# The gated convolution of a decoder trunk: c and v gates with activations held and 512 features streamed, the product turned through DRAM, and the b gate moved behind them

## The chip, the cores and the metric

The kernel runs on one core of one Trainium2 chip. The metric is device time in microseconds (us) of one execution; the median of three runs of the kernel before is 950.28 us (950.25 to 950.47). Five engines work from in-order instruction queues and meet at semaphores: TensorE (PE in the profile, its weight loads PEld), VectorE (DVE), ScalarE (ACT), GpSimd (POOL) and SyncE (SP), which here issues nearly all transfers.

## The reference

One sequence of 256 tokens with 1024 features passes two layers. Each is a half-step SwiGLU FFN (2816 hidden), a mixer, and a second half-step FFN, each behind an RMS norm and added to the residual `h`. The mixer of the second layer is a sparse attention, which the change does not touch; that of the first is the short gated convolution:

```python
def short_conv_mixer(x, w_in, conv_w, w_out):
    b_gate, c_gate, v = jnp.split(x @ w_in, 3, axis=-1)
    u = c_gate * v
    y = lax.conv_general_dilated(u, conv_w[:, None, :], window_strides=(1,),
                                 padding=[(CONV_WIDTH - 1, 0)], ...
                                 feature_group_count=D_MODEL)
    return (b_gate * y) @ w_out
```

`x` is the RMS-normed `h`; `w_in` is 1024 x 3072, and the convolution has three taps per feature, which look back over 0, 1 and 2 tokens. Everything is float32.

## The kernel before, in words

**Products.** A float32 product is made of float32r parts: each operand is split into a rounded high half and the low rest, and hi·hi, lo·hi and hi·lo are summed in PSUM. Weights come from DRAM in chunks of 128x2048 floats (`ws`, three buffers), and each half of a chunk is one *unit* of 128x1024: ACT casts it to the high half `wh` (L166), DVE subtracts to the low half `wl` (L183). Six units of each can be ready ahead. `W.take()` hands out the next one, `W.done()` says that PE is through with one and lets the stream *pump* the next (a cast on ACT, a subtraction on DVE) at that point of both queues.

**Two forms of a product.** In the *token form* (`ffn_tokens`, L432 to L434) the activations are held in the array, 128 tokens at a time, and 512 features of the weights stream past; the result has tokens on partitions. In the *feature form* (`a_pass`, L351 and L356) 128x128 weights are held and both halves of the activations, 512 wide, stream past (L351), then the high half alone, 256 wide, past the low weights (L356); the result has features on partitions, 256 tokens on the free axis.

**The convolution.** The residual lies with features on partitions, so in the kernel before all three gates are made in the feature form, for 128 features `f` at a time: eight rounds, each of three PSUM banks (c, v and b), three units of weights and 24 + 24 matmuls. After each round `conv_evac` makes what the next product needs: ACT copies and DVE adds the two halves of c and v (L365, L366), POOL multiplies them and scales by the squared inverse RMS (L718, L719), ACT and DVE do the same for b (L721, L722), POOL scales it (L723), ACT and DVE apply the taps (L727 to L729), DVE multiplies by b (L731), and `split` (L359 on ACT, L360 on DVE) leaves the two halves `zs[f]`. Between these steps `weave` pumps weights, so their casts and subtractions stand among them in the queues.

**After it.** `out_proj(zs, 1.0, nm)` is a feature-form product with four PSUM banks at its head: on the first three columns `zs[0]` to `zs[6]` are used, on the fourth `zs[0]` and `zs[1]`, and only then `zs[7]` and the rest (`cut = (7, 7, 7, 2)`). So PE asks for `zs[6]` six matmuls after the head's start, and for `zs[7]` when all 23 + 23 matmuls of the head are done.

**What sets the order.** The order is written out by hand in Python: every engine takes its instructions in the order in which the program text issues them, and a stream pump stands exactly where `W.done`, `W.pump`, `W.high` or `W.low` is called. All transfers named here stand in SP's one queue.

## Time and profile before

| what | us |
|---|---|
| median of the runs | 950.28 |
| the profiled execution, its own time | 950.93 |
| its span, first to last instruction | 949.1 |
| PE busy in the span | 944.6 |
| DVE busy | 657.5 |
| ACT busy | 532.4 |
| POOL busy | 138.8 |
| convolution's three gates on PE | 186.33 to 253.30 |
| head of its output product on PE | 253.30 to 264.45 |

Busy times are unions, so overlapping instructions of an engine count once. The last two rows are from the chain of waits, whose pieces follow each other without overlap; a matmul's own duration in other views is longer than the step from one to the next, since matmuls are pipelined. Steps from start to start are read from the timeline. Positions in us count from the start of the span.

### The profile page before, as it was taken

The page shows a single profiled execution, that of the slowest core. Times are in us where ns is not written, and L with a number is a line of the kernel's source. Part 1 is how long each engine was busy: PE and PEld are TensorE (multiplying, and loading weights), DVE is VectorE, ACT ScalarE, POOL GpSimd, SP SyncE. Part 2 cuts the span into 40 slices and gives each one's busy share as a digit, 9 for nine tenths or more (in the row PEclk, how much of TensorE's full clock was granted, in tenths as well). Part 3 has the DMA queues.
Part 4 walks back from the last instruction along what each step waited for, and adds up shares of the span by engine and source line. Part 5 has one row for each costly group of instructions (what it writes and reads, how often), then busy time and mean ns, then how long its engine had stood idle before and what let it go on. Part 6 is the DMA issues. An engine that isn't in the chain of part 4 may idle for free.

```text
span 949.1 us, 12899 instructions
## 1 busy us (share of the span) xinstructions
PE 944.6 (100%) x4674; PEld 792.3 (83%) x4674; DVE 657.5 (69%) x1058; ACT 532.4 (56%) x895; POOL 138.8 (15%) x215
## 2 busy tenths in 40 slices
PE   9999999999999999999999999999999999999998
PEld 7888888888888888888888888888877888888887
DVE  7766665778896677647756676865679786776662
ACT  7554544555565455545647774644589764544450
POOL 2000000244520010001221022200238120000000
PEclk9999999999999999999999999999999999999999
DMA  7778876645546998777646977876511247998770
GB/s 312 237 228 279 253 258 219 228 171 200 181 165 233 267 292 253 225 269 222 222 159 207 276 229 248 271 251 191 212 50 32 103 177 233 275 284 260 232 268 23
DMA packets 154380, 206.35 MB, mean 217 GB/s; under 512 B 115740, under 2 KB 131228, under 8 KB 133837
## 3 DMA queue, kind: packets, MB, share of 16 engines
q1 hardware_dynamic: 154172, 205.27, 66.3%
q8 instruction: 37, 0.61, 0.2%
q10 hardware_dynamic: 144, 0.26, 0.1%
q14 instruction: 27, 0.21, 0.1%
HBM read 189.75 MB, written 15.24 MB: 216 GB/s over the span
## 4 chain that ended last, share of the span: by engine, by line
PE 99%; DMA 1%; ACT 0%; SPq 0%; issue 0%; DVE 0%
PE mm L432 16%; PE mm L434 16%; PE mm L433 16%; PE a L533 7%; PE mm L351 4%; PE a L351 4%; PE a L539 4%; PE mm L493 3%; PE mm L494 3%; PE mm L495 3%; PE a L592 2%; PE a L590 2%; PE a L591 2%; PE mm L656 2%; PE a L356 2%; PE mm L356 2%
## 5 line engine op out<-in xcount | busy, mean ns | idle before, releaser
L183 DVE TENSOR_TENSOR wl<-ws,wh 128x1024 fp32r<-128x1024 f32 x316 | 390.5, 1255 | 209.4 <-ACT wh L166 192.2
L166 ACT CAST wh<-ws 128x1024 fp32r<-128x1024 f32 x316 | 324.6, 1048 | 219.7 <-DMA ws<-in_ffn_w_in_dram 99.0
L432 PE MATMUL mm<-wh,xs 128*128 128x512 f32 x656 | 256.2, 391 | 0.0
L434 PE MATMUL mm<-wl,xs 128*128 128x512 f32 x656 | 255.7, 390 | 0.0
L433 PE MATMUL mm<-wh,xs 128*128 128x512 f32 x656 | 255.6, 390 | 0.0
L434 PEld LDWEIGHTS mm<-wl,xs 128*128 128x128 f32 x656 | 123.2, 188 | 26.2 <-DVE wl L183 0.4
L433 PEld LDWEIGHTS mm<-wh,xs 128*128 128x128 f32 x656 | 123.3, 188 | 25.2
L432 PEld LDWEIGHTS mm<-wh,xs 128*128 128x128 f32 x656 | 123.3, 188 | 25.1
L311 POOL TENSOR_TENSOR sq<-sq,t 128x256 f32<-128x256 f32 x42 | 34.8, 829 | 384.6 <-ACT t L309 383.9
L390 ACT ACTIVATE t<-mm,rc 128x256 f32<-128x256 f32 x86 | 40.6, 472 | 56.2 <-DVE t L391 47.6
L533 PE MATMUL a<-act,wh 128*128 128x512 f32 x296 | 69.5, 390 | 0.0
L533 PEld LDWEIGHTS a<-act,wh 128*128 128x128 f32 x296 | 55.0, 188 | 10.9
L391 DVE SCALAR_TENSOR_TENSOR t<-mm,rc,t 128x256 f32<-128x256 f32 x86 | 41.4, 482 | 15.5 <-ACT t L390 12.0
L493 PE MATMUL mm<-wh,act 128*128 128x512 f32 x132 | 51.4, 390 | 0.0
L494 PE MATMUL mm<-wh,act 128*128 128x512 f32 x132 | 51.4, 389 | 0.0
L495 PE MATMUL mm<-wl,act 128*128 128x512 f32 x132 | 51.4, 389 | 0.0
L359 ACT CAST act<-t 128x256 fp32r<-128x256 f32 x96 | 34.6, 405 | 26.3 <-DVE t L731 19.4
L294 ACT ACTIVATE xs<-base 128x256 fp32r<-128x256 f32 x48 | 24.1, 505 | 43.0 <-DVE base L455 27.3
L392 DVE STREAM_TRANSPOSE t<-t 128x256 f32<-128x256 f32 x88 | 39.2, 445 | 3.1
L360 DVE TENSOR_TENSOR act<-t,act 128x256 fp32r<-128x256 f32 x96 | 37.1, 424 | 4.4 <-ACT act L359 4.4
L539 PEld LDWEIGHTS a<-act,wl 128*128 128x128 f32 x296 | 37.2, 192 | 1.0
L539 PE MATMUL a<-act,wl 128*128 128x256 f32 x296 | 37.5, 283 | 0.0
(279 smaller groups left out, 1203.6 us busy)
## 6 DMA issues: line engine op xcount, KB each, us to landing
ws<-in_ffn_w_in_dram SPq DMA_DIRECT2D x84, 1024.0 KB, 5.7
ws<-in_ffn_w_out_dram SPq DMA_DIRECT2D x44, 1024.0 KB, 6.2
ws<-in_conv_w_in_dram SPq DMA_DIRECT2D x12, 1024.0 KB, 4.6
turn<-t SPq DMA_DIRECT2D x44, 256.0 KB, 2.2
t<-turn SPq DMA_DIRECT2D x44, 256.0 KB, 7.2
ws<-in_w_kv_dram SPq DMA_DIRECT2D x6, 1024.0 KB, 5.8
ws<-in_conv_w_out_dram SPq DMA_DIRECT2D x4, 1024.0 KB, 5.0
ws<-in_attn_w_q_dram SPq DMA_DIRECT2D x4, 1024.0 KB, 4.9
```

Source lines behind the costliest of these rows:

```text
L166: ac.copy(h, src)
L183: ve.tensor_tensor(out=l, in0=src, in1=h.bitcast(F32), op=ALU.subtract)
L351: pe.matmul(o, u[0][:, k * P:(k + 1) * P], xs[k], start=(k == 0), stop=False)
L391: ve.scalar_tensor_tensor(out=s, in0=o[tt][:, T:], scalar=rc[:, tt:tt + 1], in1=s, op0=ALU.mult, op1=ALU.mult)
L432: pe.matmul(o[tt], sh, wh, start=(k == 0), stop=False)
L433: pe.matmul(o[tt], sl, wh, start=False, stop=False)
L434: pe.matmul(o[tt], sh, wl, start=False, stop=(k == 7))
L493: pe.matmul(o[:, tt], sh, wh, start=(k == 0), stop=False)
L494: pe.matmul(o[:, tt], sl, wh, start=False, stop=False)
L495: pe.matmul(o[:, tt], sh, wl, start=False, stop=(k == NF - 1))
L533: pe.matmul(o, run[k][0], lhs[k], start=(k == 0), stop=(k == last))
L539: pe.matmul(o[:, :T], run[k][1], lhs[k][:, :T], start=False, stop=(k == last))
```

## The change

The c and v gates are now made in the token form, 512 features at a time, in four groups: c of features 0 to 511, v of the same, then c and v of features 512 to 1023. ACT copies the two banks of c out (L787). DVE multiplies v's banks by them and by the squared inverse RMS of each token (L735), turns 32x32 blocks (L737), and SP writes the result to DRAM and reads it back with features on partitions (L738, L745). The inverse RMS is still made as a row (L331); for the token scale its first row goes through DRAM into a column (L768, L769), and POOL squares that (L770). Taps (L756 on ACT, L758 twice on DVE) and the scaling by the inverse RMS (L760 on POOL) follow from the turned `u`: features 0 to 511 during the fourth group, the rest behind the matmuls of b's rounds 4 to 6. The b gate then runs in the feature form alone, eight rounds of one bank, one unit and 8 + 8 matmuls. The weights are packed to fit, and two of the attention's bias rows are loaded by one transfer in place of two.

```diff
-    def conv_evac(f, ocv, ob, R, R2, zs):
-        r = total(ocv, 2)
-        yield
-        u = mk([P, 768], "pr", 6)[:, :T + 2]
-        po.memset(u[:, :2], 0.0)
-        po.tensor_tensor(out=u[:, 2:], in0=r[:, 0], in1=r[:, 1], op=ALU.mult)
-        po.tensor_tensor(out=u[:, 2:], in0=u[:, 2:], in1=R2, op=ALU.mult)
...
+    def conv_tokens(o, step):
+        for k in range(8):
+            if k % 2 == 0:
+                u, = W.take()
+            wh, wl = [u[x][:, (k % 2) * 512:(k % 2 + 1) * 512] for x in range(2)]
+            for tt in range(2):
+                sh, sl = xs[k][:, tt * P:(tt + 1) * P], xs[k][:, T + tt * P:T + (tt + 1) * P]
+                pe.matmul(o[:, tt], sh, wh, start=(k == 0), stop=False)
+                pe.matmul(o[:, tt], sl, wh, start=False, stop=False)
+                pe.matmul(o[:, tt], sh, wl, start=False, stop=(k == 7))
+            if k % 2 == 1:
+                W.done()
+            step(k)
+    def conv_turned(gate, o):
+        d = mk([2, 2, P, T], "conv", 2, pool=dr)
+        for tt in range(2):
+            tb = t2()
+            ve.scalar_tensor_tensor(out=gate[tt], in0=o[:, tt], scalar=conv["r2"][:, tt:tt + 1], in1=gate[tt],
+                                    op0=ALU.mult, op1=ALU.mult)
+            ve.transpose(tb, gate[tt])
+            sy.dma_start(d[:, tt].rearrange("m p n -> p m n"), tb.rearrange("p (m n) -> p m n", m=2))
+        return d
+    def conv_placed(d):
+        r = []
+        for m in range(2):
+            r.append(t2([P, 2, T]))
+            sy.dma_start(r[m].rearrange("p c (b j) -> p c b j", j=32),
+                         d[m].rearrange("t (b i) (x c j) -> (i x) c (t b) j", i=32, c=2, j=32))
+        return r
+    def conv_taps(f):
+        m, c = divmod(f, 2)
+        if c == 0:
+            Y.append(act([P, 2, T], F32))
+        tap = [gt[:, G_CONV + 8 * a + f:G_CONV + 8 * a + f + 1] for a in range(3)]
+        u, y = conv["u", m // 2][m % 2][:, c], Y[m][:, c]
+        ac.activation(y, u, AF.Copy, scale=tap[2])
+        for a in range(2):
+            ve.scalar_tensor_tensor(out=y[:, 2 - a:], in0=u[:, :T - 2 + a], scalar=tap[a], in1=y[:, 2 - a:],
+                                    op0=ALU.mult, op1=ALU.add)
+        po.tensor_tensor(out=y, in0=y, in1=conv["R"], op=ALU.mult)
+        if f % 4 == 3:
+            del conv["u", m // 2]
+    def conv_step(n, k):
+        if n == 0 and k == 5:
+            conv["R"] = R = nm.rows()
+            rd, rc, conv["r2"] = mk([1, T], "rd", 1, pool=dr), mk([P, 2], "rc", 2, pool=tiny), sm([P, 2])
+            sy.dma_start(rd, R[:1])
+            sy.dma_start(rc, rd.rearrange("o (t p) -> (o p) t", t=2))
+            po.tensor_tensor(out=conv["r2"], in0=rc, in1=rc, op=ALU.mult)
+        if n == 1 and k == 1:
+            next(tab)
+        if n == 2 and k == 3:
+            conv["u", 0] = conv_placed(conv.pop(("d", 0)))
+        if n == 3:
+            if 3 <= k < 7:
+                conv_taps(k - 3)
+            elif k == 7:
+                next(tab)
+    for n in range(4):
+        o = bank2()
+        conv_tokens(o, lambda k: conv_step(n, k))
+        if n % 2 == 0:
+            gate = [t2() for _ in range(2)]
+            for tt in range(2):
+                ac.copy(gate[tt], o[:, tt])
+        else:
+            conv["d", n // 2] = conv_turned(gate, o)
+            del gate
+    for f in range(8):
+        o, (u,) = bank(), W.take()
+        a_pass([(o, u, xs, range(8))])
+        W.done(1, False)
+        if f == 1:
+            conv["u", 1] = conv_placed(conv.pop(("d", 1)))
+        for x in {4: (4, 5), 5: (6,), 6: (7,)}.get(f, ()):
+            conv_taps(x)
         b = t1()
-        ac.copy(b, ob[:, T:])
-        ve.tensor_tensor(out=b, in0=ob[:, :T], in1=b, op=ALU.add)
-        po.tensor_tensor(out=b, in0=b, in1=R, op=ALU.mult)
...
+        ac.copy(b, o[:, T:])
+        ve.tensor_tensor(out=b, in0=o[:, :T], in1=b, op=ALU.add)
+        W.pump(1)
+        ve.tensor_tensor(out=b, in0=b, in1=Y[f // 2][:, f % 2], op=ALU.mult)
+        zs.append(act())
+        split(b, zs[f])
+        W.pump()
...
-            if a == 0 or j < 6:
+            if a == 0 or j < 4:
```

What this does to the queues is seen at three places. The first is DVE's queue in a round of the b gate. Before, one round `f` of all three gates stood there so (`mm` holds c and v, `a` holds b, `pr` is u, `wl` a weight unit's low half, `act` the half of `zs` that DVE writes):

```order
L366 TENSOR_TENSOR t_342_1834<-mm_1785,t_342_1834 128x512
L183 TENSOR_TENSOR wl_1841<-ws_1677,wh_1837 128x1024
L722 TENSOR_TENSOR t_347_1847<-a_1784,t_347_1847 128x256
L183 TENSOR_TENSOR wl_1853<-ws_1760,wh_1851 128x1024
L728 SCALAR_TENSOR_TENSOR t_350_1855<-pr_1843,base,t_350_1855 128x256
L729 SCALAR_TENSOR_TENSOR t_350_1855<-pr_1843,base,t_350_1855 128x256
L183 TENSOR_TENSOR wl_1863<-ws_1760,wh_1859 128x1024
L731 TENSOR_TENSOR t_350_1855<-t_350_1855,t_347_1847 128x256
L360 TENSOR_TENSOR act_1866<-t_350_1855,act_1866 128x256
```

Now round 5 of the b gate stands so (`act_2208` and `act_2171` are tiles of `Y`, `t_395` is u as it came back):

```order
L758 SCALAR_TENSOR_TENSOR act_2208<-t_395_2081,base,act_2208 128x254
L758 SCALAR_TENSOR_TENSOR act_2208<-t_395_2081,base,act_2208 128x255
L801 TENSOR_TENSOR t_420_2213<-a_2191,t_420_2213 128x256
L183 TENSOR_TENSOR wl_2220<-ws_2088,wh_2216 128x1024
L803 TENSOR_TENSOR t_420_2213<-t_420_2213,act_2171 128x256
L360 TENSOR_TENSOR act_2223<-t_420_2213,act_2223 128x256
```

A round has one weight unit in place of three and a third of the matmuls; rounds 0 to 3 and 7 lack the two L758, round 4 has four of them.

The second place is DVE's queue where the v gate of the second half ends and the b gate begins. Ahead of these rows stand, for features 0 to 511, two groups of four L758 with a weight subtraction between them. Of the kernel before nothing answers to it; there the round shown first repeats.

```order
L183 TENSOR_TENSOR wl_2018<-ws_1925,wh_2014 128x1024
L272 TENSOR_TENSOR act_2021<-t_342_1788,act_2021 128x128
L735 SCALAR_TENSOR_TENSOR t_368_1929<-mm_1933,sm_1744,t_368_1929 128x512
L737 STREAM_TRANSPOSE t_386_2026<-t_368_1929 128x512
L735 SCALAR_TENSOR_TENSOR t_369_1930<-mm_1933,sm_1744,t_369_1930 128x512
L737 STREAM_TRANSPOSE t_387_2030<-t_369_1930 128x512
L801 TENSOR_TENSOR t_389_2051<-a_2034,t_389_2051 128x256
L183 TENSOR_TENSOR wl_2056<-ws_1964,wh_2054 128x1024
L803 TENSOR_TENSOR t_389_2051<-t_389_2051,act_1968 128x256
```

The evacuation of the fourth group (L735, L737) thus stands ahead of the first round of b, and the taps of the first half ahead of both.

The third place is SP's queue. Before, in this stretch it held the loads of the weights alone, one behind the other; now the second half of the turn stands among them:

```order
L139 DMA ws_2016<-in_conv_w_out_dram 128x2048
L738 DMA conv_2025<-t_386_2026 128x2x256
L738 DMA conv_2025<-t_387_2030 128x2x256
L745 DMA t_394_2079<-conv_2025 128x16x32
L745 DMA t_395_2081<-conv_2025 128x16x32
L139 DMA ws_2088<-in_conv_w_out_dram 128x2048
L139 DMA ws_2146<-in_conv_w_out_dram 128x2048
```

Three of the four chunks of the output product's weights are loaded behind the two writes and two reads.

## The prediction

> **What bounds the kernel now.** I read the page's busy shares and chain first, then the chain within the convolution, then the queues of DVE, ACT and POOL there.

> ```profile
> PE 944.6 (100%) x4674; PEld 792.3 (83%) x4674; DVE 657.5 (69%) x1058; ACT 532.4 (56%) x895; POOL 138.8 (15%) x215
> ...
> PE 99%; DMA 1%; ACT 0%; SPq 0%; issue 0%; DVE 0%
> ```

> PE is the chain nearly everywhere: what the change saves on PE is saved, and what makes PE wait is lost. The chain in the convolution, one whole round and then the head of the output product (start, us, what, count):

> ```profile
> 203.26 3.65 PE mm L351 x16
> 206.91 1.81 PE a L351 x8
> 208.72 1.91 PE mm L356 x16
> 210.64 0.96 PE a L356 x8
> ...
> 253.30 5.24 PE a L351 x23
> 258.54 2.75 PE a L356 x23
> 261.29 0.23 PE a L351
> ```

> The pieces abut: no wait. c and v cost 3.65 + 1.91 = 5.56 a round, b 1.81 + 0.96 = 2.77. A 512-wide step takes 5.24/23 = 0.228. The first matmul that needs `zs[7]` starts at 261.29. When is that half written?

> ```profile
> 260.52 0.43 DVE L360 TENSOR_TENSOR act<-t,act 128x256 fp32r<-128x256 f32 x1 [0.47 <-ACT act L359]
> ```

> At 260.95, 7.65 behind the last gate matmul's end at 253.30, and 0.34 ahead of its use. So the tail of this stage already has almost no slack: what counts is when the last `zs` are written.

> **What PE saves.** The token form stands in the next FFN; 29 steps lie between these two rows of the timeline:

> ```profile
> 278.21 0.39 PE L432 MATMUL mm<-wh,xs 128*128 128x512 f32 x1
> ...
> 284.78 0.39 PE L434 MATMUL mm<-wl,xs 128*128 128x512 f32 x1
> ```

> A step is 6.57/29 = 0.2266. c and v become 4 x 48 = 192 of them, 43.5; before they were 8 x 5.56 = 44.5. The saving is **1.0 us**: as many columns stream, in fewer matmuls. b keeps its 8 x 2.77 = 22.2, and the two row-sum matmuls stay. Call E the end of the fourth token group on PE; PE then ends b at E + 22.2 and wants `zs[6]` six steps into the head, at E + 22.2 + 1.37 = **E + 23.5**.

> **What the other engines must do by then.** The units of work, from the same stage, first DVE with POOL quiet on its scaling, then with POOL at work (start, us; starts give the steps):

> ```profile
> 200.71 0.49 DVE L728 SCALAR_TENSOR_TENSOR t<-pr,base,t 128x256 f32<-128x256 f32 x1 [1.08 <-ACT t L727]
> 201.24 0.48 DVE L729 SCALAR_TENSOR_TENSOR t<-pr,base,t 128x256 f32<-128x256 f32 x1
> 201.65 1.22 DVE L183 TENSOR_TENSOR wl<-ws,wh 128x1024 fp32r<-128x1024 f32 x1
> 202.79 0.42 DVE L731 TENSOR_TENSOR t<-t,t 128x256 f32<-128x256 f32 x1
> 203.68 0.43 DVE L360 TENSOR_TENSOR act<-t,act 128x256 fp32r<-128x256 f32 x1 [0.47 <-ACT act L359]
> ...
> 205.12 1.64 DVE L183 TENSOR_TENSOR wl<-ws,wh 128x1024 fp32r<-128x1024 f32 x1 [0.26 <-ACT wh L166]
> 206.68 0.41 DVE L722 TENSOR_TENSOR t<-a,t 128x256 f32<-128x256 f32 x1
> 207.01 1.33 DVE L183 TENSOR_TENSOR wl<-ws,wh 128x1024 fp32r<-128x1024 f32 x1
> 208.27 0.96 DVE L728 SCALAR_TENSOR_TENSOR t<-pr,base,t 128x256 f32<-128x256 f32 x1
> 209.26 0.48 DVE L729 SCALAR_TENSOR_TENSOR t<-pr,base,t 128x256 f32<-128x256 f32 x1
> ```

> ```profile
> 200.10 0.73 POOL L723 TENSOR_TENSOR t<-t,R 128x256 f32<-128x256 f32 x1
> ...
> 207.22 1.72 POOL L723 TENSOR_TENSOR t<-t,R 128x256 f32<-128x256 f32 x1
> ```

> The same tap takes 0.49 at 200.71, and 0.96 where POOL's scaling runs to 208.94; the weight subtraction 1.22 or 1.64. Each stretches POOL too, 0.73 to 1.72. Steps: two taps 201.65 - 200.71 = 0.94, or 1.39 beside POOL (0.99 + 0.40); a subtraction 1.14, or 1.56 beside POOL; the add from PSUM 0.33; the multiply 0.42 and 0.04 to ACT. The ACT side:

> ```profile
> 243.63 0.41 ACT L359 CAST act<-t 128x256 fp32r<-128x256 f32 x1 [2.74 <-DVE t L731]
> 243.94 0.29 ACT L271 CAST act<-t 128x128 fp32r<-128x128 f32 x1
> ...
> 245.58 0.37 ACT L721 COPY t<-a 128x256 f32<-128x256 f32 x1
> 245.84 1.06 ACT L166 CAST wh<-ws 128x1024 fp32r<-128x1024 f32 x1
> ```

> Split cast to the next 0.31, copy to the next 0.26, weight cast 1.05. Other pieces, from the groups of the stage (count, busy us, mean ns of one), and two transposes from the timeline:

> ```profile
> L183 DVE TENSOR_TENSOR wl<-ws,wh 128x1024 fp32r<-128x1024 f32 x23 | 31.8, 1381 | 2.3 <-ACT wh L166 2.3
> ...
> L366 DVE TENSOR_TENSOR t<-mm,t 128x512 f32<-128x512 f32 x8 | 5.5, 684 | 0.8 <-ACT t L365 0.5
> ...
> L331 DVE RECIPROCAL R<-t 128x256 f32<-128x256 f32 x1 | 1.8, 1753 | 3.1 <-ACT t L329 3.1
> ...
> L272 DVE TENSOR_TENSOR act<-t,act 128x128 fp32r<-128x128 f32 x1 | 0.3, 289 | 0.0
> ```

> ```profile
> L727 ACT ACTIVATE t<-pr,base 128x256 f32<-128x256 f32 x7 | 3.6, 510 | 8.5 <-POOL pr L719 8.5
> ```

> ```profile
> 157.83 1.31 DVE L501 STREAM_TRANSPOSE pr<-mm 128x512 f32<-128x512 f32 x2
> ```

> **DVE at E.** In the fourth token group a unit of weights is freed each 12 steps = 2.72, and its cast and subtraction stand behind that. The one freed at E - 5.44 is cast in 1.05 and subtracted in 1.22, so DVE gets to the taps at E - 3.2. From there its queue holds, with POOL scaling each finished feature (L760) beside the next instruction: taps 0.94 + 1.39, subtraction 1.56, taps 2.33, subtraction 1.56, the table's L272 0.25 (0.29, less the overlap of the next start). Sum 8.0: it is done at **E + 4.8**. Behind it stands the evacuation of the fourth group, which the trace lacks in this shape: a multiply of 128x512 from PSUM is nearest to L366, 0.72 with its step, and two transposes to L501's 1.31; 2 x 0.72 + 1.31 = 2.75. DVE comes to the first round of b at **E + 7.6**, 4.8 after PE ended that round.

> **The rounds of b.** The queues make a ring: ACT copies b (L800), casts a weight; DVE, which added the copy in the meantime, subtracts that weight, multiplies by Y (L803); ACT casts the split, and only then copies the next round, which stands behind it. One turn: 0.26 + 1.05 + 0.04 + 1.14 + 0.46 + 0.31 = **3.26**, where PE makes a round in 2.77. Before, the three weights per round ran in the shadow of 8.33 us of matmuls; now each `zs` waits for one. Rounds 5 and 6 carry one feature's taps, round 4 two: ACT's tap 0.55, taps 0.94, add 0.33, subtraction beside POOL 1.56, 0.46, 0.31 make 4.15; with a second pair at 1.39 it is 5.54.

> First split cast: E + 7.6 + 0.33 + 1.14 + 0.46 = E + 9.5. Rounds 1 to 3 add 9.8, round 4 5.5, rounds 5 and 6 8.3: E + 33.1, and 0.86 later (203.68 + 0.43 - 203.25, where ACT had begun) `zs[6]` is whole: **E + 34.0**. PE waits 34.0 - 23.5 = **10.5 us** in the head, in pieces, since `zs[4]` and `zs[5]` are late too. `zs[7]` comes one turn later, 3.3, behind 17 x 0.228 + 2.75 = 6.6 of matmuls: covered.

> **Costed at nothing.** The scale's column: it is asked for by DVE at the end of the second group, 21.8 after the start; R starts at 36 steps, 8.2, and has a square root, the reciprocal's 1.75 and two small transfers to pass. Transfers of the turn's shapes (KB, median us to landing):

> ```profile
> back<-pr SPq DMA_DIRECT2D x6, 256.0 KB, 2.2
> t<-back SPq DMA_DIRECT2D x6, 256.0 KB, 6.0
> ```

> At about 2.2 each that is near 8.2 + 3 + 4.4 = 16, so 6 us of cover; gone, DVE would stall. On SP two waits stand ahead of weight loads, but six ready units are 16 us of PE. The turn's transfers: `back` and its return are the same shapes; the second half is written at E + 7.6 + 2.2, back 6.0 later, by E + 16 or, with a second issue held up, E + 20; its taps start at E + 19.6. ACT's copies of c (L787) run behind a whole group. The bias edit moves one transfer that only POOL awaits.

> **Sum.** -1.0 + 10.5 = **+9.5**. The span goes from 949.1 to 958.6, that execution from its own 950.93 to 960.4; it lies 0.65 above the median shown, so the median goes from 950.28 to **959.8**.

> **Bounds.** Lower: POOL never in the way. Three tap pairs and five subtractions up to `zs[6]` lose 0.45 and 0.42 each, 3.45: a wait of 7.0, +6.0, 956.3. Upper: the second half of the turn comes late as well (below) and every plain subtraction takes the stage's mean of 1.38: 0.16 more in four rounds, 0.6, with the full lock's 2.4 (below) and the transfer's 1.6: +14.1, 964.4. I take the middle, since the contended rows are this stage's own.

> **Rivals.** *The wait is absorbed.* DVE's whole work in the convolution hardly changes, and PE has four banks for b: if what DVE owes at E were worked off earlier, PE would keep its pace and only the saving would show: 949.3, within 0.2% (1.9 us, about what a measurement of this kernel can tell from no change). Against it: the ring alone, with no debt and no taps, puts `zs[6]` at E + 2.8 + 1.9 + 6 x 3.26 + 0.86 = E + 25.1, a wait of 1.6 and +0.6. It decides only where the ring turns in under 3.0.

> *A full lock.* If DVE stood still for the whole of POOL's instruction, 0.73, and not the 0.45 that rows lose, eight collisions would add 8 x 0.3 = 2.4: +11.9, 962.2. For it: POOL's 1.72 contains a DVE instruction entire. Against: 0.96 - 0.49 = 0.47. [...]

> *The turn is late.* The reads are the longest issues on SP:

> ```profile
> L508 SPq DMA_DIRECT2D t<-back x6: 591/1834/4294, 161.8 to 653.0; - x6
> ...
> DMA to landing us min/median/max: 2.1/5.1/7.1
> ```

> If the second read of the second half is issued 4.3 late and lands after 7.1, it is there at E + 9.8 + 4.3 + 7.1 = E + 21.2, 1.6 behind the time when its taps could start: +11.1, 961.4. Against: only round 5's features lie in that tile.

> **Chances.** Forecast as summed, between the bounds: 0.72. Full lock 0.10, turn late 0.08, both on the slow side. Absorbed to within 0.2%: 0.05; faster, where PE's step in the token form fell further than the FFN's: 0.03; the ring alone, +0.6, is within the 0.05; 0.02 for a larger loss that I don't see. Slower 0.92, same 0.05, faster 0.03. Range 955.5 to 964.0.

> **What would show it.** Right: in the chain, PE waits in L351 of the head for `act` from DVE, some 10 us in three or four pieces; DVE first comes to L801 some 7 to 8 after the fourth group's end; L803 to L803 is 3.2 to 3.3 in rounds 1 to 3, 4 to 5.6 in rounds 4 to 6; the token groups take 10.9 each. Wrong: no such wait in the head, PE waiting in a token group for weights or a bank, or DVE waiting for a transfer in L756 or L758.

## The result: 12.3 us slower, where 9.5 were forecast

The changed kernel takes 962.65 us (median of four runs, 961.83 to 963.21), the kernel before 950.38 beside it: a ratio of 1.0128 (95% interval 1.0110 to 1.0146). The forecast was 959.8, in a range of 955.5 to 964.0. The profiled execution took 962.77 (its span is 961.0), 11.84 more than the execution profiled before (950.93). From here on the working goes by these two.

The page, its busy shares and its row of the granted clock:

```profile
PE 948.0 (99%) x4610; PEld 791.2 (82%) x4610; DVE 655.0 (68%) x1058; ACT 532.6 (55%) x891; POOL 111.1 (12%) x191
...
PEclk9999999999899999999999999999999999999999
```

PE's busy time went up, though it has 64 matmuls fewer (4674 before), and one slice of the clock's row is no longer a 9. First the stage's borders, from PE's timeline, where c's first token matmul, b's first matmul and the head stand:

```profile
186.15 0.40 PE L724 MATMUL mm<-wh,xs 128*128 128x512 f32 x1
...
229.96 1.98 PE L351 MATMUL a<-xs,wh 128*128 128x512 f32 x8
...
232.73 0.63 PE L351 MATMUL a<-xs,wh 128*128 128x512 f32 x2
...
251.33 1.11 PE L356 MATMUL a<-xs,wl 128*128 128x256 f32 x8
252.61 1.21 PE L351 MATMUL a<-act,wh 128*128 128x512 f32 x4 [0.17 <-DVE t L801]
255.46 0.79 PE L351 MATMUL a<-act,wh 128*128 128x512 f32 x1 [1.64 <-DVE act L360]
259.66 0.80 PE L351 MATMUL a<-act,wh 128*128 128x512 f32 x1 [3.40 <-DVE act L360]
263.83 6.53 PE L351 MATMUL a<-act,wh 128*128 128x512 f32 x17 [3.38 <-DVE act L360]
270.20 2.92 PE L356 MATMUL a<-act,wl 128*128 128x256 f32 x23
```

The same two borders in the kernel before:

```profile
186.17 0.63 PE L351 MATMUL mm<-xs,wh 128*128 128x512 f32 x2
...
252.18 1.12 PE L356 MATMUL a<-xs,wl 128*128 128x256 f32 x8
253.13 0.63 PE L351 MATMUL a<-act,wh 128*128 128x512 f32 x2
```

E is 229.96. The first round of b takes 232.73 - 229.96 = 2.77, the seven behind it 2.79 each: the last one's low products begin at 251.33 and need 0.95 (before, 252.18 to 253.13), so that without a wait the head would begin at 252.28. That is 66.13 behind the stage's start, where the kernel before needed 66.96: a saving of 0.83. PE wants `zs[6]` 1.37 later, at 253.65, and goes on at 263.83: it lost 10.18. And then something that no step of the forecast holds: the 17 matmuls behind the last wait take 270.20 - 263.83 = 6.37, 0.375 a step in place of 0.228, which is 2.49 more than 3.88. The sum: -0.83 + 10.18 + 2.49 = **11.84**, the whole difference. From 270.20 on the steps are those of before.

DVE's queue from the fourth group on, from its timeline:

```profile
226.77 2.27 DVE L758 SCALAR_TENSOR_TENSOR act<-t,base,act 128x254 f32<-128x254 f32 x4
228.97 1.21 DVE L183 TENSOR_TENSOR wl<-ws,wh 128x1024 fp32r<-128x1024 f32 x1
230.10 2.75 DVE L758 SCALAR_TENSOR_TENSOR act<-t,base,act 128x254 f32<-128x254 f32 x4
232.78 1.21 DVE L183 TENSOR_TENSOR wl<-ws,wh 128x1024 fp32r<-128x1024 f32 x1
233.91 0.83 DVE L272 TENSOR_TENSOR act<-t,act 128x128 fp32r<-128x128 f32 x1
234.66 0.74 DVE L735 SCALAR_TENSOR_TENSOR t<-mm,sm,t 128x512 f32<-128x512 f32 x1
...
237.45 0.38 DVE L801 TENSOR_TENSOR t<-a,t 128x256 f32<-128x256 f32 x1
...
238.89 0.41 DVE L803 TENSOR_TENSOR t<-t,act 128x256 f32<-128x256 f32 x1
...
248.64 0.42 DVE L803 TENSOR_TENSOR t<-t,act 128x256 f32<-128x256 f32 x1
...
254.10 0.41 DVE L803 TENSOR_TENSOR t<-t,act 128x256 f32<-128x256 f32 x1
...
258.29 0.41 DVE L803 TENSOR_TENSOR t<-t,act 128x256 f32<-128x256 f32 x1
...
263.35 0.43 DVE L360 TENSOR_TENSOR act<-t,act 128x256 fp32r<-128x256 f32 x1 [0.47 <-ACT act L359]
```

DVE is done with what it owes at 234.66 (E + 4.7), begins the first round of b at 237.45 (E + 7.5), turns a round in 3.25 (9.75 for three, 238.89 to 248.64), round 4 in 5.46, round 5 in 4.19, and `zs[6]` is whole at 263.78, **E + 33.8**.

What happened to the 17 matmuls stands in the table by stretches, with cuts at the points where the clock changed (the stretch and its length, busy us of PE, PEld, DVE, ACT and POOL with counts, then the granted clock, then two columns on transfers; an instruction that reaches over a cut is counted on both sides):

```profile
251.89:255.30 3.41, 1.76 (x9) 1.02 (x7) 2.94 (x5) 0.76 (x3) 0.78 (x2) 1.00 0.59 235
255.30:258.71 3.41, 0.79 (x1) 0.29 (x1) 3.37 (x6) 1.26 (x3) 0.72 (x1) 0.50 0.01 2
...
262.12:265.54 3.42, 1.71 (x4) 1.43 (x5) 2.49 (x5) 1.62 (x3) 0.00 (x0) 0.50 0.09 36
265.54:268.95 3.41, 3.41 (x9) 2.63 (x9) 1.01 (x3) 0.40 (x1) 0.00 (x0) 0.50 0.59 187
268.95:272.36 3.41, 3.41 (x25) 3.15 (x24) 0.00 (x0) 0.00 (x0) 0.00 (x0) 1.00 0.29 120
```

TensorE's granted clock fell to 0.50 at 255.30, during the first of PE's long waits, and came back at 268.95, 5.12 after the last of them had ended. In the stretch of 3.41 that is wholly at work and wholly at half clock, 9 matmuls are counted, where 3.41 holds 15 steps of 0.228; their starts, in narrow windows of the timeline, lie 0.43 apart (264.42, 264.85, 265.27).

### The profile page after: what moved, and what is told of

It is laid out like the page before. It is cut to its first block, busy times and chain, and to the rows that moved or that the text cites. A ratio compares the mean times of both kernels' runs of the same rounds, so it can differ in the third digit from the quotient of the medians.

```text
span 961.0 us, 12779 instructions
## 1 busy us (share of the span) xinstructions
PE 948.0 (99%) x4610; PEld 791.2 (82%) x4610; DVE 655.0 (68%) x1058; ACT 532.6 (55%) x891; POOL 111.1 (12%) x191
## 4 chain that ended last, share of the span: by engine, by line
PE 95%; DVE 2%; issue 1%; ACT 1%; DMA 0%; DVEq 0%; ACTq 0%
PE mm L432 16%; PE mm L434 16%; PE mm L433 15%; PE a L533 7%; PE a L539 4%; PE mm L495 3%; PE mm L493 3%; PE mm L494 3%; PE a L351 2%; PE mm L656 2%; PE a L590 2%; PE a L591 2%; PE a L592 2%; PE mm L725 1%; PE mm L724 1%
## 5 line engine op out<-in xcount | busy, mean ns | idle before, releaser
L183 DVE TENSOR_TENSOR wl<-ws,wh 128x1024 fp32r<-128x1024 f32 x316 | 388.5, 1248 | 221.1 <-ACT wh L166 207.0
L166 ACT CAST wh<-ws 128x1024 fp32r<-128x1024 f32 x316 | 325.1, 1048 | 238.4 <-DMA ws<-in_ffn_w_in_dram 93.6
L432 PE MATMUL mm<-wh,xs 128*128 128x512 f32 x656 | 255.9, 390 | 0.0
L434 PE MATMUL mm<-wl,xs 128*128 128x512 f32 x656 | 255.4, 389 | 0.0
L434 PEld LDWEIGHTS mm<-wl,xs 128*128 128x128 f32 x656 | 123.2, 188 | 26.3 <-DVE wl L183 0.4
L432 PEld LDWEIGHTS mm<-wh,xs 128*128 128x128 f32 x656 | 123.2, 188 | 25.1
L359 ACT CAST act<-t 128x256 fp32r<-128x256 f32 x96 | 34.5, 404 | 23.4 <-DVE t L803 18.9
L360 DVE TENSOR_TENSOR act<-t,act 128x256 fp32r<-128x256 f32 x96 | 37.0, 423 | 3.8 <-ACT act L359 3.8
## 6 DMA issues: line engine op xcount, KB each, us to landing
turn<-t SPq DMA_DIRECT2D x44, 256.0 KB, 2.3
t<-turn SPq DMA_DIRECT2D x44, 256.0 KB, 7.1
```

What stands on the lines that cost most here:

```text
L166: ac.copy(h, src)
L183: ve.tensor_tensor(out=l, in0=src, in1=h.bitcast(F32), op=ALU.subtract)
L432: pe.matmul(o[tt], sh, wh, start=(k == 0), stop=False)
L434: pe.matmul(o[tt], sh, wl, start=False, stop=(k == 7))
```

## Experiments

### Is it the clock? The waits filled

Dummy matmuls, which wait for nothing and whose results nobody reads, stand ahead of the matmuls that wait.

```diff
+            spare = bank2()
...
+                    if c == 0 and factor == 1.0:
+                        for x in range({4: 7, 5: 14, 6: 14}.get(k, 0)):
+                            pe.matmul(spare[:, x % 2], lhs[0][:, :P], lhs[0], start=True, stop=True)
```

> Dummy work in the waits: in the output product's head, 7, 14 and 14 matmuls that wait for nothing (zs[0] against zs[0] into a spare bank, results unused) stand ahead of the three matmuls of the first column that wait for zs[4], zs[5] and zs[6]. They are sized to the three waits of the changed kernel (35 x 0.228 = 8.0 us of work in 1.64 + 3.40 + 3.38 us of waiting). Theory 'clock': the 17 head matmuls behind the last wait took 0.384 us a step because the granted clock had fallen to 0.5 while PE idled; kept busy, PE stays at full clock, the 17 steps go back to 0.23, and the time falls by 2.65 from 962.65 to about 960.0 (959.5 to 961, if a dummy overruns its wait a little). Rival 'not the clock': the 17 slow steps come from something else that runs then (DVE, ACT or transfers beside PE); the steps stay at 0.38 and the time at 962.6 or up to 1 more.

Measured: 960.18 us, 2.47 less. PE's timeline (L483 are the dummies, L484 the head):

```profile
259.83 3.38 PE L483 MATMUL mm<-act 128*128 128x512 f32 x14
263.69 4.19 PE L484 MATMUL a<-act,wh 128*128 128x512 f32 x17 [0.48 <-DVE act L360]
267.72 2.92 PE L488 MATMUL a<-act,wl 128*128 128x256 f32 x23
```

`zs[6]` comes when it came before, and the 17 steps behind it take 4.03 in place of 6.37, beside the same work of DVE and ACT. That PE idled is what made them slow: 35 matmuls more made the kernel 2.47 faster.

The same with the third wait left idle:

```diff
-                        for x in range({4: 7, 5: 14, 6: 14}.get(k, 0)):
+                        for x in range({4: 7, 5: 14}.get(k, 0)):
```

> As the run with dummy work in all three waits, but the third wait (3.4 us, for zs[6]) is left idle: 7 and 14 dummy matmuls ahead of the first two. Theory 'clock, on a grid of 3.41': one idle stretch of 3.4 always holds a grid point behind which the clock is 0.5, and it stays there for two grid steps, 6.8, at the least; 3.4 to 6.8 of that lie behind the wait's end, so that half of them is lost: 1.0 to 2.5 beside the 960.2 of the full dummies, 961 to 962.7. Rival 'only long or repeated idling counts': the 17 steps behind it stay at 0.23 to 0.25, 960.2.

Measured: 962.71 us, all of it lost again. PE's timeline, and the stretches between the changes of the clock:

```profile
263.72 6.58 PE L484 MATMUL a<-act,wh 128*128 128x512 f32 x17 [3.67 <-DVE act L360]
```

```profile
258.69:262.10 3.41, 0.86 (x3) 0.19 (x1) 2.99 (x5) 1.96 (x4) 0.72 (x1) 1.00 0.83 298
262.10:265.51 3.41, 1.79 (x4) 1.49 (x5) 2.48 (x5) 1.62 (x3) 0.00 (x0) 0.50 0.03 10
265.51:268.92 3.41, 3.41 (x9) 2.65 (x8) 0.94 (x3) 0.40 (x1) 0.00 (x0) 0.50 0.66 223
```

One wait of 3.67 ahead of matmuls without a wait costs the 17 steps as much as three waits did (270.14 - 263.72 = 6.42, beside 6.37): half clock for 6.83, of which 5.2 lie behind the wait's end.

### What makes `zs[6]` late: the debt, the ring, the collisions

Each of the next four kernels takes one part away. First DVE's taps (y is then one tap of the convolution alone):

```diff
-        for a in range(2):
-            ve.scalar_tensor_tensor(out=y[:, 2 - a:], in0=u[:, :T - 2 + a], scalar=tap[a], in1=y[:, 2 - a:],
-                                    op0=ALU.mult, op1=ALU.add)
```

> Without DVE's taps: the two L758 are left out, so that y is only the third tap times u (one third of the convolution is computed). ACT's tap and POOL's scaling stay. Theory 'DVE's debt and the ring': up to zs[6], seven features' taps are gone from DVE's path: about 1.88 + 2.27 + 2.75 ahead of the second half's evacuation count only beyond the time PE gives DVE anyway, and 0.94 to 1.4 in each of rounds 4 to 6. zs[6] comes about 8 to 9 us earlier than E + 33.9, but not before the ring alone allows it (E + 25.1 to E + 26.5), so 1.6 to 4 us of waiting are left of 10.3; the clock stays up or falls briefly. Time 953 to 957. Rival 'the transfers of the turn or of the weights set the end': taking DVE's work away changes little, 960 or more.

Measured: 957.39 us, 5.3 less and just outside of what was expected. DVE's timeline (L735 the evacuation, L800 the multiply by Y; here E is 229.66):

```profile
230.72 1.45 DVE L183 TENSOR_TENSOR wl<-ws,wh 128x1024 fp32r<-128x1024 f32 x1 [1.49 <-ACT wh L166]
...
232.29 0.74 DVE L735 SCALAR_TENSOR_TENSOR t<-mm,sm,t 128x512 f32<-128x512 f32 x1
...
236.52 0.41 DVE L800 TENSOR_TENSOR t<-t,act 128x256 f32<-128x256 f32 x1
...
239.77 0.42 DVE L800 TENSOR_TENSOR t<-t,act 128x256 f32<-128x256 f32 x1
...
258.51 0.43 DVE L360 TENSOR_TENSOR act<-t,act 128x256 fp32r<-128x256 f32 x1 [0.47 <-ACT act L359]
```

A debt remains without taps: the last weight of the group is cast by ACT only after PE has freed its unit, and its subtraction stands ahead of the evacuation, which begins at E + 2.6. The ring still turns in 3.25, and in rounds 4 to 6 ACT's taps lengthen it. `zs[6]` is whole at E + 29.3: DVE's taps and what POOL does to them are 4.5 of the 10.2. The expectation had left out the weight's 2.6 and ACT's taps.

Then POOL's scaling (y is not scaled by the inverse RMS):

```diff
-        po.tensor_tensor(out=y, in0=y, in1=conv["R"], op=ALU.mult)
```

> Without POOL's scaling: L760 is left out, so that y is not scaled by the inverse RMS of its token. Everything else stays. Theory 'partial loss, 0.45 a collision' (the prediction's): the eight collisions on DVE's path vanish, 3.4 us; the wait falls from 10.3 to about 7, and the time to 959.2, or to 956.6 to 957 if the shorter waits keep the clock up too. Rival 'full lock' (POOL's whole 0.73 or more each): 5.8 us gone, the wait 4.5, 954 to 957. Rival 'POOL does not matter': 962 or more.

Measured: 958.57 us, 4.1 less. `zs[6]` is whole at 260.10, E + 30.2 (here E is 229.87) in place of E + 33.8; for the eight collisions on the way that is 0.45 each. Rows of POOL and of DVE in the changed kernel, and of DVE without the scaling, show how a collision goes:

```profile
229.19 1.59 POOL L760 TENSOR_TENSOR act<-act,R 128x256 f32<-128x256 f32 x1 [0.43 <-ACT act L756]
...
252.37 0.73 POOL L760 TENSOR_TENSOR act<-act,R 128x256 f32<-128x256 f32 x1 [0.42 <-DVE act L758]
```

```profile
252.48 1.70 DVE L183 TENSOR_TENSOR wl<-ws,wh 128x1024 fp32r<-128x1024 f32 x1
```

```profile
232.61 0.29 DVE L272 TENSOR_TENSOR act<-t,act 128x128 fp32r<-128x128 f32 x1
...
250.27 1.22 DVE L183 TENSOR_TENSOR wl<-ws,wh 128x1024 fp32r<-128x1024 f32 x1
```

POOL's instruction of 252.37 holds until 253.10 and is not stretched; DVE's subtraction, begun at 252.48 with 0.62 of it to go, takes 0.48 more than the 1.22 without POOL. The other way round, POOL's instruction of 229.19 begins while DVE subtracts (228.97 to 230.18, quoted above at its full speed of 1.21), and needs 1.59. So in both pairs the one that came first kept its pace, and the other lost most of what was left of it: DVE 0.48 with 0.62 to go, POOL 1.59 - 0.73 = 0.86 with 0.99 to go. DVE's 0.48 is less than the whole 0.73 of POOL's instruction.

Then the ring, with every instruction kept and only the order of a round changed:

```diff
-        W.pump(1)
...
-        split(b, zs[f])
-        W.pump()
+        ac.copy(zs[f][:, :T], b)
+        W.low()
+        ve.tensor_tensor(out=zs[f][:, T:], in0=b, in1=zs[f][:, :T].bitcast(F32), op=ALU.subtract)
+        W.high()
+    W.low()
```

> The ring of a b round broken: ACT's weight cast comes at a round's end, behind the split cast, one round ahead, and DVE's weight subtraction between the split cast and the split subtraction, so that neither stands between the copy of b and the multiply. Same instructions, other order. Theory 'ring': a round no longer takes 3.25 us in rounds 1 to 3 but what DVE alone needs (0.33 + 0.42 + 1.14 + 0.41 = 2.3 to 2.8, PE's own 2.77 where DVE has caught up), zs[6] comes about 2.7 to 4 us earlier, and the time falls to 958.5 to 960, or by up to 2.65 more if the waits get short enough for the clock to stay up. Rival 'DVE's debt alone': rounds stay at 3.2, since DVE is never idle in them, and the time stays at 962 to 963.

Measured: 959.56 us, 3.1 less. DVE's timeline, the adds of rounds 1 and 2 (E is 229.28):

```profile
239.37 0.42 DVE L801 TENSOR_TENSOR t<-a,t 128x256 f32<-128x256 f32 x1 [0.80 <-ACT t L800]
...
242.01 0.43 DVE L801 TENSOR_TENSOR t<-a,t 128x256 f32<-128x256 f32 x1 [0.22 <-ACT t L800]
```

A round takes 2.64, less than PE's 2.79, and the first begins where it did, at E + 7.5. PE loses 7.45 in place of 10.18. Rounds of 3.25 were the order's, not DVE's load.

Last the debt, with the taps of features 0 to 3 earlier in the fourth group:

```diff
-            if 3 <= k < 7:
-                conv_taps(k - 3)
+            if k < 4:
+                conv_taps(k)
```

> Debt alone, smaller: the taps of features 0 to 3 stand at the steps k = 0 to 3 of the fourth token group in place of 3 to 6, so that 4.1 us of PE's work more lie between them and the group's end. Same instructions. Theory 'debt': DVE, which came to the fourth group's evacuation 4.8 after E, still has the two weight subtractions of that group and the table's step ahead of it, so that only the taps (2.27 + 2.75, less what waits there) move out: it comes 1.5 to 3 earlier, zs[6] comes as much earlier, and the time falls from 962.65 to 960 to 961. The rounds keep their 3.25, the head keeps waits of over 1.5 each, and the granted clock still falls to 0.5 for a multiple of 3.41 (it lasted 13.65, 6.79, 10.24 and 10.23 in the changed kernel and in the runs without taps, without scaling and with the ring broken). Rival 'ring alone': DVE's late start is made up in the rounds, nothing changes, 962 to 963.

Measured: 960.04 us, 2.6 less. The evacuation begins at 232.12 (E + 2.8, since E is 229.35 here; without taps it was E + 2.6), the rounds keep their 3.25, PE loses 8.26, and the clock is down for two stretches of 3.41 in place of four, so that the 17 steps take 5.54. In the stretches by the changes of the clock stands one more thing:

```profile
250.99:254.40 3.41, 2.28 (x13) 1.44 (x11) 2.90 (x7) 2.02 (x4) 0.35 (x1) 1.00 0.00 0
254.40:257.81 3.41, 0.50 (x1) 0.19 (x1) 2.90 (x5) 1.59 (x4) 0.37 (x1) 1.00 0.30 55
257.81:261.22 3.41, 0.00 (x0) 0.00 (x0) 2.94 (x6) 1.26 (x4) 0.72 (x1) 0.50 0.61 252
```

The first stretch, with PE at work for 2.28 of 3.41, is not followed by half clock; the one with 1.76 in the changed kernel was.

### All of it undone with the change kept

If debt, ring and clock are the whole loss, an order that avoids them must bring back the time of before, with c and v still in the token form. The taps go to two early steps of the fourth group, the subtractions of that group's last two weights are put off, and the rounds take the order of the ring experiment; taps 4 to 7 stand behind a round's split. Beside that the table's second step moves a group ahead, the turned `u` is read back a round earlier, and the head first lets the stream go on by two units.

```diff
+        if n == 2 and k == 7:
+            next(tab)
+        if n == 3 and k in (1, 3):
+            conv_taps(k - 1)
+            conv_taps(k)
...
+                if late and k > 4:
+                    W.done(1, False)
+                    W.high()
...
+        conv_round(f, f in (0, 1, 2, 4, 7))
+        for x in {3: (4, 5), 4: (6,), 5: (7,)}.get(f, ()):
+            conv_taps(x)
+        W.high()
```

(`late` is true in the fourth group; `conv_round` is multiply, split cast, where its second argument says so a put-off weight subtraction, split subtraction.)

> Debt and ring together: taps of features 0 to 3 at k = 1 and 3 of the fourth group; the table's second step a group earlier; the subtractions of the last two weights of that group put off into the rounds; in a round ACT casts the split before the next weight, and the put-off subtractions stand in rounds 0, 1, 2, 4 and 7; taps 4 and 5 behind round 3, 6 behind 4, 7 behind 5, each behind the round's split. Same instructions and the same result. Theory 'debt and ring': DVE comes to the fourth group's evacuation at about E + 0.5, the rounds take 2.3 to 3 us, zs[6] is there within 0 to 2 of PE's asking for it, no wait is over 1.5, the clock stays at 1.0, and what is left is the saving on PE of 1.0 and the rest of the wait: 949.3 to 951.5, not to be told from the kernel before (950.6 on this chip) or within 0.2% of it. Rival 'something else holds the end too' (the turn's transfers, a weight load, POOL's scaling as a wait): waits of 3 or more remain, 953 or more.

Measured: 951.24 us against 950.58, a ratio of 1.0006 (0.9997 to 1.0015). PE's timeline of the head:

```profile
252.10 1.55 PE L351 MATMUL a<-act,wh 128*128 128x512 f32 x6
254.40 4.15 PE L351 MATMUL a<-act,wh 128*128 128x512 f32 x17 [0.75 <-DVE act L803]
258.38 3.14 PE L356 MATMUL a<-act,wl 128*128 128x256 f32 x23
```

Of 10.2 lost, 0.9 is left (254.40 against 252.10 + 1.37), the clock is 1.00 throughout, and of the 2.49 0.1 is left: 254.40 to 258.38 is 3.98. Moving taps 4 and 5 behind round 2:

```diff
-        conv_round(f, f in (0, 1, 2, 4, 7))
-        for x in {3: (4, 5), 4: (6,), 5: (7,)}.get(f, ()):
+        conv_round(f, f in (0, 1, 3, 4, 7))
+        for x in {2: (4, 5), 4: (6,), 5: (7,)}.get(f, ()):
```

> As the last one, but taps 4 and 5 stand behind round 2 and the put-off subtractions in rounds 0, 1, 3, 4 and 7, so that round 3 carries no taps and zs[4] is not behind them. Theory 'debt and ring': 0.0 to 0.5 better than the last one, 949.3 to 951, if u of the second half is back by then (its reads end at about E + 14, round 2 ends at about E + 11 to 12, so here ACT's tap could wait 2 to 3 us for the transfer). Rival 'turn late': that wait stands ahead of the next round's copy on ACT and comes back in the head, 951.5 to 953.

Measured: 951.07 us, ratio 1.0006 (0.9997 to 1.0014), no difference to the last one that these runs could tell. The turned `u` is there in time even one round earlier. Lastly PE's order in the head, so that `zs[6]` is asked for later:

```diff
+            for c in range(3):
+                highs(c, range(6))
+            highs(3, range(2))
+            for c in range(3):
+                highs(c, (6,))
```

> The second of the two spread versions, and PE's order in the output product's head changed: the three first columns take zs[0] to zs[5], then the fourth column zs[0] and zs[1], then the three take zs[6]; the low products of the fourth column follow with its other matmuls. Same matmuls. PE asks for zs[6] 20 steps into the head in place of 6, 3.2 us later, where it waited 0.6 for it; the fourth column's bank and low weights come 0.2 later than asked so far and are asked for later too. Theory 'debt and ring were the whole loss': no wait is left, and the saving of 1.0 on PE shows: 949.5 to 950.2, 0.4 to 1.1 below the kernel before. Rival 'the banks': the three columns' banks come free with the rounds 4 to 6, and a wait for one takes the place: 951.

Measured: 950.54 us against 950.53, ratio 0.9999 (0.9991 to 1.0008). PE's timeline (L481 and L485 are the head's high and low products):

```profile
252.39 5.41 PE L481 MATMUL a<-act,wh 128*128 128x512 f32 x23
257.64 0.98 PE L485 MATMUL a<-act,wl 128*128 128x256 f32 x7
258.88 2.24 PE L485 MATMUL a<-act,wl 128*128 128x256 f32 x14 [0.26 <-DVE wl L183]
260.96 0.40 PE L481 MATMUL a<-act,wh 128*128 128x512 f32 x1
```

Neither `zs` nor a bank is waited for any more; now PE waits for the low halves of the output product's weights, whose subtractions were put off. Its 21 low products take 260.96 - 257.64 = 3.32, where 23 took 2.75 before, so 21 would take 2.51: 0.81 more, as much as the saving of 0.83. So the saving does not show: DVE's work around E was moved from one thing that PE needs to another, and the rival that was expected, the banks, is not what took its place. No version here beats the kernel before.

## Why the prediction was right in its steps and short in its sum

**The saving** of 1.0 is 0.83: b's eight rounds, kept at 8 x 2.77 in the forecast, took 22.32. **The debt**: DVE came to the taps at E - 3.2, as worked out, and was through at E + 4.7 (4.8). The parts behind that sum cancel: both subtractions, priced at 1.56 beside POOL, ran at their own 1.21, since each began while POOL was idle (228.97 and 232.78, POOL's next at 229.19 and 233.00); the second four taps took 2.68 to the next start, priced at 2.33, and the table's L272 0.75, priced at 0.25, since POOL's last scaling, held up by a subtraction, ran into it (its own duration is 0.83, without POOL 0.29). The collisions were counted well and placed wrongly. **The evacuation**, which no row of before showed, took 237.45 - 234.66 = 2.79; the two neighbours gave 2.75.

**The ring** of 3.26 was 3.25, its rounds with taps 5.46 and 4.19 (5.54 and 4.15), `zs[6]` whole at E + 33.8 (34.0), the wait 10.18 (10.5). That the order of the two queues sets this, and not DVE's load, is shown by the ring experiment; that the debt sets the start, by the two on taps. **What was costed at nothing** held: the longest read of the turn landed after 5.6, and DVE waited for none.

**The step that failed is the sum, -1.0 + 10.5.** It counts a wait at its own length and lets PE go on behind it at 0.228 a step, as the sentence on `zs[7]` has it ("behind 17 x 0.228 + 2.75"). The 17 steps took 0.375 each: a term of 2.49 was missing. It is the clock, since filling the waits removes it and opening one of them brings it back. No row quoted from the kernel before has a wait of PE, so its price could not be read there; but that PE would idle in three pieces was forecast, and what idling does to the clock was not asked. The upper bound of 964.4 took the result in, with terms (the lock, a late transfer, dearer subtractions) of which none occurred: that the range holds the result is luck.

**The rivals.** The full lock forecast 962.2, nearly the time that came, and is refuted all the same: it needs `zs[6]` at E + 36.4, and it came at 33.8. That DVE loses time beside POOL holds (1.70 against 1.22); no run shows its price of the whole 0.73, nor the 2.4 made of it: the loss was 0.48 in that pair, and 0.45 each over the eight collisions. The row quoted for it was misread: POOL's 1.72, 207.22 to 208.94, contains no DVE instruction entire, since the subtraction beside it had begun before it, at 207.01. A time that fits is no evidence for a mechanism; the row in which it must show is. The late turn is refuted by the rows of DVE and ACT, none of which waits for a transfer there. That the wait is absorbed did not happen by itself; the reordered kernel shows that it can be, to within 0.9, and that the saving is then spent on late weights.

## What to carry to other kernels

Price a new wait on PE with two terms, its own length and slower matmuls behind it (in the changed kernel a granted clock of 0.50 and 0.375 a step in place of 0.228; the waits were 1.6 to 3.7 in the runs here, and one of 0.9, in the reordered kernel, cost no clock); where the wait cannot be removed, dummy matmuls that wait for nothing can give the second term back, as the 2.47 here. Before a gate is moved to the end of a stage, write down what DVE still owes at that point and what one turn of the ACT-DVE ring takes with the order as written: those two sums gave the wait to 0.3 us here. Putting work off on the engine that owes it only pays if nobody on PE needs that work soon.

## What the runs showed of the hardware that was not expected

So the price of idling is not proportional to it here: after 10.2 lost in three waits the 17 steps took 6.37, after one wait of 3.67 with short ones of 0.17 and 0.51 ahead of it 6.42, and in the other runs with half clock between 1.6 (without taps, 258.99 to 264.42) and 3.0 (ring broken, 260.41 to 267.28) more than 3.88. Where the grid falls differs between executions: the first record lies 6.13 us behind the span's start in the trace of the changed kernel, 4.66 in that of the kernel before. Executions of one kernel differ in the clock too. Of the changed kernel's four, two show a mean granted clock of 0.993, which four stretches give, and two 0.995, which fits three; with one wait left idle, three of 962.67 to 962.80 us show 0.996 and the one of 961.72 us 0.998, which fits one stretch in place of two. The two grid steps "at the least" of that run's expectation were an estimate from the runs before it, whose shortest stretch was 6.83.
